# Two-layer hybrid decoder step: pooling and GLU columns as plain blocks, the gates as sevenfold products, and stores taken off the load queue

## The chip, the cores and the metric

The kernel runs on one core of a Trainium2 chip. The time is device microseconds of one execution of the whole program, read as the median of several runs; smaller is better. The engines are named as in the profile: PE is TensorE (matmul) and PEld its weight loads, DVE is VectorE, ACT is ScalarE, POOL is GpSimd, SP is SyncE, which here only issues DMAs. A name with a q (SPq, POOLq) is the engine's own DMA queue.

## The reference

One layer is applied to 1024 prompt tokens with 16 learned meta tokens ahead of them, and to 8 x 8 sample tokens, which carry their own states.

```python
h = rmsnorm(x)
a_val, a_gate, a_silu, p_in, p_silu, g_a, g_b = split(h @ w_in)     # seven groups of 1024 columns
u = a_val * sigmoid(a_gate)                                         # GLU
c = silu(layernorm(depthwise_conv(u, width=31) + conv_b)) * silu(a_silu)
br_a = c @ w_conv_out
pooled = trailing_mean(p_in, windows 2/4/8/16 by channel group) - p_in
q = (pooled @ w_pool_mix per group) * pool_scale * silu(p_silu)
br_b = q @ w_pool_out
y = rmsnorm(x + (sigmoid(g_a) * br_a + sigmoid(g_b) * br_b) @ w_out)
```

All is float32. The kernel also returns the last 30 GLU outputs and the last 15 pooling inputs as new states.

## The kernel before

**Layout.** Channels lie on the 128 partitions, tokens along the free axis. The 1104 tokens are cut into two halves of 552 (8 meta, 512 prompt, 32 sample). Each float32 operand of a matmul is split into a rounded high part and a low rest, and three matmuls (high-high, high-low, low-high) stand for one.

**Two ways to make a column group.** A column group is 128 output columns of `w_in`; there are 56. A *plain block* multiplies the group's 8 slices of 128 input channels with both token halves: 8 slices x 3 x 2 matmuls per half, 96 matmuls in all. A *sevenfold pair* makes two column groups at once with 7 products in place of 8 (the Strassen-Winograd scheme over 2 token halves x 2 halves of the channels x 2 column groups): each product is 4 slices x 3 x 2 = 24 matmuls, 168 for the pair instead of 192. It needs sums of weights (q3, q2, q1, q4) and sums of inputs (T1 to T4), and two combinations of results on DVE (`c4` and `c2`, lines 461 and 470). The product called `d` overwrites PSUM tile `v`, so it has to wait until DVE has read `v` for `c4`.

**The stages.** (1) Pooling columns p0 to p5 as plain blocks, while the RMS factor is worked out; their results go unscaled to DRAM (`d_raw`). (2) 25 sevenfold pairs: p3 (columns p6 and p7), g0 to g3 with v0 to v3 (GLU gates and values), and 16 pairs of gates q, b, a, s; `ORDER` gives the order. (3) `pmix`: the pooled channels times the group maps. (4) `ppo`: pool projection. LayerNorm statistics of the convolution are made beside it. (5) `pco`: conv projection and merge. (6) `pwo`: output projection and the final norm.

**What DVE does beside stage 2.** The pooling windows (`pool_window`) and the convolution (`conv_chunk`: for each of 8 channel chunks 31 taps over 1024 prompt tokens, and small sums for the sample tokens). These are kept in a list `todo`, and `fill` places as many of them between the products as a planned clock (3.0 us per product) leaves room for. The order on every engine is fixed when the program is written; each engine runs its own list in order and waits at semaphores.

**Weights of a product.** `prepare` loads a quarter of a pair's weights 8 products ahead on SP, adds a second quarter with an accumulating DMA from POOL 6 ahead (for q3 and q1), makes q2 and q4 on DVE 5 ahead, and splits 4 ahead with `split_dma`: two copies on ACT, then an accumulating DMA from POOL that subtracts the rounded part. All plain loads and all stores are issued by SP, in the order in which the program wrote them, a store as soon as its ACT instruction is written.

Of the kernel before, what the change touches and what calls it, by code (L numbers as in the profile page):

```python
# [65 lines left out]
def hybrid_trunk_kernel(  # L66
# [87 lines left out]

    def refine(r, a, t):
# [47 lines left out]
    d_raw = dram.tile([NX, P, 2, HT], F32, name="d_raw")  # L203
# [99 lines left out]
    d_rms = dram.tile([P, 2, HT], F32, name="d_rms")  # L303
    sp.dma_start(out=d_rms, in_=rms)
    keep_raw(0, 1, outs[0])

    t_ops = {}

    def t_split(name, k, src, how):
        t = slot(f"t{name}{k}", (2, HT), F32R)
        t_ops.setdefault(name, []).append(t)
        how(t[:, 0], t[:, 1], src)

    xa, xb = xs[:NQ], xs[NQ:]
    for k in range(NQ):
        dve.scalar_tensor_tensor(xa[k], xa[k], col(OFF_NG, k), rms, ALU.mult, ALU.mult)  # L320
        t_split("11", k, xa[k][:, 0], split)
        dve.scalar_tensor_tensor(xb[k], xb[k], col(OFF_NG, NQ + k), rms, ALU.mult, ALU.mult)
# [3 lines left out]
    for k in range(NQ):  # L326

        dve.tensor_tensor(xa[k][:, 0], xa[k][:, 0], xa[k][:, 1], ALU.subtract)
        dve.tensor_tensor(xa[k][:, 1], xb[k][:, 1], xa[k][:, 1], ALU.subtract)
        t_split("T3", k, xa[k][:, 1], split)  # L330
    plain1(3)
    plain1(4)
    plain1(5)
    keep_raw(2, 1, outs[2])

    def more_t(step):
        for k in range(NQ):
            if step == 0:
                t_split("21", k, xb[k][:, 0], split_dma)
            elif step == 1:  # L340
                dve.scalar_tensor_tensor(xa[k][:, 1], xa[k][:, 0], -1.0, xb[k][:, 1], ALU.mult, ALU.subtract)
                t_split("T2", k, xa[k][:, 1], split_dma)
            elif step == 2:
                t_split("T1", k, xa[k][:, 0], split)
            elif step == 3:
                t_split("22", k, xb[k][:, 1], split_dma)
            else:
                dve.scalar_tensor_tensor(xa[k][:, 1], xa[k][:, 1], -1.0, xb[k][:, 0], ALU.mult, ALU.subtract)
                t_split("T4", k, xa[k][:, 1], split)
# [3 lines left out]
    clock = {"pe": 0.0, "dve": 0.0}  # L353
# [16 lines left out]


    class Weights:
        def __init__(self, src, name):
            self.name = name
            (self.a_, self.b_), (self.c_, self.d_) = ((x[:, :NQ], x[:, NQ:]) for x in src)
            self.raw, self.op = {}, {}

        def load(self, what):
            src, key = {
                "a": (self.a_, "a"),  # L380
                "q3": (self.a_, "q3"),
                "q2": (self.c_, "q1"),
                "b": (self.b_, "b"),
                "d": (self.d_, "d"),
            }.get(what, (None, None))
            if key:
# [3 lines left out]
        def add(self, what):  # L390
            key, src = {"q3": ("q3", self.c_), "q2": ("q1", self.d_)}.get(what, (None, None))
            if key:
                pool.dma_start(out=self.raw[key], in_=src, accum_op=ALU.add)

        def sum(self, what):
            x, y = {"q2": ("q1", "a"), "q4": ("q2", "b")}.get(what, (None, None))
            if x:
                self.raw[what] = half_raw(f"{what}_{self.name}")
                dve.tensor_tensor(self.raw[what], self.raw[x], self.raw[y], ALU.add)
                spend(512)  # L400

        def split(self, what):
            o = op_tile(f"wo{what}_{self.name}", (2, NQ, P))
            split_dma(o[:, 0], o[:, 1], self.raw[what])
# [4 lines left out]
    def prepare(t):  # L409
        for lead, f in (  # L410
            (LEAD_LOAD, Weights.load),
            (LEAD_ADD, Weights.add),
# [7 lines left out]
    def product(out, w, t, units, first, last):  # L420
# [3 lines left out]
        clock["pe"] += T_PRODUCT  # L424
# [61 lines left out]


    def pool_window(j, e, es):
        sp.dma_start(out=o_pp[j], in_=e[:, TP - PB : TP])
        sp.dma_start(out=o_ps[j], in_=es[:, :, DS:])  # L490
        w = WINDOWS[j // 2]
        cur = [e, es]

        def step(d):
            lo = 2 * d - 1
            s, ss = cur
            cur[0] = slot(f"pw{j}_{d}", (TP,))
            cur[1] = st.tile([P, DB, PS], F32, tag="pws", name=f"pws{j}_{d}")
            dve.tensor_tensor(cur[0][:, lo:], s[:, lo:], s[:, lo - d : TP - d], ALU.add)
            dve.tensor_tensor(cur[1][:, :, lo:], ss[:, :, lo:], ss[:, :, lo - d : PS - d], ALU.add)  # L500

        work = []
        d = 1
        while d < w:
            work.append((t_op(TP) + t_op(DB * PS), lambda d=d: step(d)))
            d *= 2

        def last():
            s, ss = cur
            dve.scalar_tensor_tensor(e[:, META:], s[:, META:], 1.0 / w, e[:, META:], ALU.mult, ALU.subtract)  # L510
# [577 lines left out]
```

## Time and profile before

| what | value |
|---|---|
| median of 3 runs (lowest to highest) | 1257.62 us (1257.25 to 1264.47) |
| profiled execution: its own time, its span | 1264.1 us, 1262.3 us |
| PE, DVE, ACT, POOL busy | 1001.3, 719.7, 536.4, 278.4 us |
| mean granted TensorE clock | 0.888 |
| stage 1 | 0 to 81.9 us |
| stage 2 | 81.9 to 851 us |
| pmix, ppo, pco, pwo begin | 859, 905, 1040, 1158 us |

The page of the profile gives shares of the whole span, which mix the six stages. The table by stretch (busy time of every engine, granted clock, share of the 16 DMA engines' time) is the one to start from; then, for a stretch in which PE is not busy, the list of who waited for whom. A wait is put down to whatever came last, so a wait of PE for DVE has to be followed to what DVE waited for. In the 40 slices of the page PE is near full in the first two, at 1 to 7 tenths in the next eight, and at 5 to 9 from there on.

### The profile page before, as it was taken

What the parts mean: (1) busy time and instruction counts of PE and PEld (TensorE: products, weight loads), DVE (VectorE), ACT (ScalarE), POOL (GpSimd) and SP (SyncE); (2) the same over time, 40 slices, a digit from 0 to 9 for tenths busy, and PEclk for the clock granted to TensorE, in tenths of its full rate; (3) what the DMA queues carried; (4) which work ended last, traced back from release to release, by engine and by line L of the source; (5) the groups of instructions that cost most, each with busy time, mean ns of one, the idle gap of its engine ahead of it and who ended that gap; (6) DMA issues with size and microseconds to landing.
All of it is one profiled execution on the core that took longest, in us unless ns stands there. A gap on an engine that the chain in (4) does not pass through costs nothing. (4 is left out here: it accounts for less than half of the span.)

```text
span 1262.3 us, 18203 instructions
## 1 busy us (share of the span) xinstructions
PE 1001.3 (79%) x6960; PEld 967.7 (77%) x6960; DVE 719.7 (57%) x901; ACT 536.4 (42%) x928; POOL 278.4 (22%) x340
## 2 busy tenths in 40 slices
PE   9952516745898979898899879895897665999997
PEld 9952516634897979898889879895797665999885
DVE  6462335234796879676987689752624343446333
ACT  7535425333454555454545346441423543314111
POOL 0004233222333333333333333310011111100000
PEclk9986758767888989998999889897899787999999
DMA  7119889898989799979897989969962667855222
GB/s 259 63 62 191 197 152 181 197 173 168 235 213 206 126 231 220 217 133 214 198 234 113 216 180 230 212 165 352 354 168 81 175 166 192 244 144 185 86 81 100
DMA packets 146711, 230.66 MB, mean 183 GB/s; under 512 B 47936, under 2 KB 49344, under 8 KB 146624
## 3 DMA queue, kind: packets, MB, share of 16 engines
q1 hardware_dynamic: 104288, 149.98, 38.3%
q0 software_dynamic: 42336, 79.53, 36.7%
q8 instruction: 54, 0.88, 0.3%
q14 instruction: 33, 0.27, 0.1%
HBM read 116.77 MB, written 50.18 MB: 132 GB/s over the span
## 5 line engine op out<-in xcount | busy, mean ns | idle before, releaser
L606 DVE SCALAR_TENSOR_TENSOR c<-ce,pv,c 128x1024 f32<-128x1024 f32 x240 | 307.9, 1283 | 6.5
L146 PE MATMUL pco<-cx,w_co 128*128 128x272 f32 x768 | 101.7, 296 | 21.5 <-DMA w_co<-raw_co 10.8
L146 PEld LDWEIGHTS pco<-cx,w_co 128*128 128x128 f32 x768 | 100.5, 195 | 22.7 <-DMA w_co<-raw_co 11.3
L146 PE MATMUL ppo<-q,w_po 128*128 128x272 f32 x768 | 102.4, 297 | 5.5 <-DMA w_po<-raw_po 5.5
L146 PEld LDWEIGHTS ppo<-q,w_po 128*128 128x128 f32 x768 | 101.9, 197 | 6.0 <-DMA w_po<-raw_po 6.0
L961 PE MATMUL pwo<-wo,mx 128*128 128x512 f32 x336 | 79.2, 394 | 0.0
L961 PEld LDWEIGHTS pwo<-wo,mx 128*128 128x128 f32 x336 | 63.1, 188 | 14.7
L146 PE MATMUL pp<-xg,wh_p 128*128 128x276 f32 x384 | 65.9, 292 | 1.0 <-ACT rawp L242 0.6
L146 PEld LDWEIGHTS pp<-xg,wh_p 128*128 128x128 f32 x384 | 55.1, 189 | 2.5 <-DVE xg L195 0.9
L146 PE MATMUL pmix<-lp,m 128*128 128x272 f32 x192 | 33.3, 339 | 21.1 <-DMA lp<-d_pool 9.3
L146 PEld LDWEIGHTS pmix<-lp,m 128*128 128x128 f32 x192 | 31.0, 235 | 23.3 <-issue 16.2
L123 POOL DMA_DIRECT2D w_po<-raw_po x16 | 13.9, 867 | 140.1 <-ACT w_po L122 99.4
L550 DVE TENSOR_TENSOR pe<-lraw,lrms 128x512 f32<-128x512 f32 x12 | 8.3, 692 | 62.0 <-DMA lrms<-d_rms 62.0
L848 DVE TENSOR_TENSOR lb<-ppo,lb 128x544 f32<-128x544 f32 x16 | 11.5, 722 | 55.0 <-DMA lb<-d_sgb 41.7
L146 PE MATMUL pp<-xg,wl_p 128*128 128x276 f32 x192 | 40.0, 289 | 0.0
L146 PE MATMUL px_q<-tT,woq_q 128*128 128x272 f32 x192 | 28.3, 307 | 11.0 <-ACT c_q L437 10.7
L116 ACT CAST mx<-lga 128x544 fp32r<-128x544 f32 x16 | 10.3, 646 | 62.0 <-DVE lga L923 62.0
L943 ACT ACTIVATE sq<-xr 128x1024 f32<-128x1024 f32 (+1 forms) x9 | 8.7, 965 | 64.1 <-DVE xr L980 64.1
L146 PEld LDWEIGHTS px_q<-tT,woq_q 128*128 128x128 f32 x192 | 27.0, 206 | 11.4 <-ACT c_q L437 10.9
L146 PE MATMUL px_v<-tT,woq_v 128*128 128x276 f32 x192 | 28.1, 306 | 8.6 <-ACT c_v L437 8.6
L146 PEld LDWEIGHTS px_v<-tT,woq_v 128*128 128x128 f32 x192 | 27.2, 205 | 8.8 <-ACT c_v L437 8.8
L980 DVE TENSOR_TENSOR xr<-pwo,xr 128x1024 f32<-128x1024 f32 (+1 forms) x9 | 10.0, 1106 | 40.0 <-PE pwo L961 25.8
(414 smaller groups left out, 2417.5 us busy)
## 6 DMA issues: line engine op xcount, KB each, us to landing
d_pool<-poolop SPq DMA_DIRECT2D x16, 544.0 KB, 3.4
lp<-d_pool SPq DMA_DIRECT2D x16, 544.0 KB, 7.5
d_c<-c SPq DMA_DIRECT2D x8, 544.0 KB, 3.5
lg<-d_gate SPq DMA_DIRECT2D x16, 272.0 KB, 6.7
lb<-d_sgb SPq DMA_DIRECT2D x16, 272.0 KB, 6.4
lc<-d_c SPq DMA_DIRECT2D x8, 544.0 KB, 10.5
d_tb<-lb SPq DMA_DIRECT2D x16, 272.0 KB, 2.6
lsa<-d_sa SPq DMA_DIRECT2D x16, 272.0 KB, 6.9
```

Of the source, the lines that this page charges most:

```text
L116: act.copy(dst_h, src)
L123: pool.dma_start(out=dst_l, in_=src, accum_op=ALU.add)
L146: pe.matmul(out[:, u, : hi - lo], w(k, a), xs(k, b)[:, lo:hi], start=first and k == ks[0] and i == 0, stop=last and k == ks[-1] and i == 2 ...
L550: dve.tensor_tensor(o[1], r[1], f[1], ALU.mult)
L606: dve.scalar_tensor_tensor(c, s, wk[:, k : k + 1], c, ALU.mult, ALU.add)
L848: dve.tensor_tensor(of_half(lb[h]), ps, of_half(lb[h]), ALU.mult)
L943: act.activation(sq[:rows, c], xr[:, c], AF.Square, accum_out=a1 if ns[0] else a0)
L961: pe.matmul(ps[:, n - ns[0]], x(k), wo[k][n][w], start=(k == 0 and s == 0), stop=(k == NK - 1 and s == len(passes) - 1),)
L980: dve.tensor_tensor(v3(xr[:, c], 512), ps[:, : len(ns)], v3(xr[:, c], 512), ALU.add)
```

## The change

- Stage 2 becomes two phases. `BLOCKS`: p6, p7 and then g0, v0, ... g7, v7, 18 plain blocks. `ORDER`: the 16 pairs of gates stay sevenfold. The matmuls of stage 2 go from 25 x 168 = 4200 to 18 x 96 + 16 x 168 = 4416.
- Both token halves of the normalized input are split whole (`hx`, 16 tiles); T1 to T4 are made at the end of the blocks.
- A GLU result is not copied into the convolution's input by ACT and POOL: DVE multiplies, the result goes to DRAM (`d_e`, `d_es`), and `Conv.fetch` loads it back, at most two chunks at a time.
- The pooling work is planned in `todo` with everything it does; `d_rms` is gone, the RMS factor stays in SBUF; raw columns are loaded one chunk ahead (`pool_load`).
- All sums of weights are made on DVE (q3, q1, q2, q4) from four loaded quarters; the accumulating POOL loads are gone. q4 is split by ACT and DVE.
- Results of gates, `d_raw` and p columns are stored from ACT's queue. The other stores stay on SP, but `defer` writes them 1 to 3 steps later in the program.
- The first loads of pmix are written before the end of the last pair, and the stores of `d_tb` in ppo one half later.

Cut to its core:

```diff
-ORDER = "p3 g0 q0 q1 q2 g1 q3 b0 b1 g2 b2 b3 a0 g3 a1 a2 a3 s0 s1 s2 s3"
-LEAD_LOAD, LEAD_ADD, LEAD_SUM, LEAD_SPLIT = 8, 6, 5, 4
+BLOCKS = "p6 p7 " + " ".join(f"g{i} v{i}" for i in range(8))
+ORDER = "q0 q1 q2 q3 b0 b1 b2 b3 a0 a1 a2 a3 s0 s1 s2 s3"
+LEAD_LOAD, LEAD_SUM, LEAD_SPLIT = 8, 5, 4
+ON_DVE = ("q4",)
...
+    def defer(steps, run):
+        due.append((clock["step"] + steps, run))
+    def step(us):
+        clock["step"] += 1
+        clock["pe"] += us
+        for x in [x for x in due if x[0] <= clock["step"]]:
+            due.remove(x)
+            x[1]()
...
     def keep_raw(j, h, ps):
...
-        sp.dma_start(out=d_raw[j][:, h], in_=z)
+        act.dma_start(out=d_raw[j][:, h], in_=z)
...
+            self.src = {"a": ("a", a), "q3": ("c", c), "q2": ("d", d), "b": ("b", b)}
...
-        def add(self, what):
-            key, src = {"q3": ("q3", self.c_), "q2": ("q1", self.d_)}.get(what, (None, None))
-            if key:
-                pool.dma_start(out=self.raw[key], in_=src, accum_op=ALU.add)
         def sum(self, what):
-            x, y = {"q2": ("q1", "a"), "q4": ("q2", "b")}.get(what, (None, None))
+            sums = {"q3": (("q3", "a", "c"),), "q2": (("q1", "c", "d"), ("q2", "q1", "a")), "q4": (("q4", "q2", "b"),)}
+            for key, x, y in sums.get(what, ()):
+                self.raw[key] = half_raw(f"{key}_{self.name}")
+                dve.tensor_tensor(self.raw[key], self.raw[x], self.raw[y], ALU.add)
...
+            if what in ON_DVE:
+                split(o[:, 0], o[:, 1], self.raw[what])
+            else:
+                split_dma(o[:, 0], o[:, 1], self.raw[what])
...
             act.activation(o, z, func)
-            sp.dma_start(out=dst[2 * i + b][:, h], in_=flat(o))
+            act.dma_start(out=dst[2 * i + b][:, h], in_=flat(o))
...
+        else:                                   # a GLU value block
+            z = sg.pop(h)
+            dve.tensor_tensor(v3(z, HT // 2), ps, v3(z, HT // 2), ALU.mult)
+            def out():
+                sp.dma_start(out=d_e[i][:, META + h * HP : META + (h + 1) * HP], in_=p)
+                sp.dma_start(out=d_e[i][:, h * HM : (h + 1) * HM], in_=m)
+                sp.dma_start(out=d_es[i][:, h * DB // 2 : (h + 1) * DB // 2], in_=s)
+            defer(1, out)
...
+        def fetch(self):
+            sp.dma_start(out=e[:, CB:], in_=d_e[i])
+            sp.dma_start(out=es[:, :, :CB], in_=sconv[i])
+            sp.dma_start(out=es[:, :, CB:], in_=d_es[i])
+            defer(3, lambda: sp.dma_start(out=o_cp[i], in_=e[:, TP : TP + CB]))
...
+    for n, (kind, i) in enumerate(blocks):
+        if n + 2 < len(blocks):
+            ops[n + 2].load()
+        if n + 1 < len(blocks):
+            ops[n + 1].split()
+        if left in (3, 2):
+            make_t(3 - left, split_dma)
...
+            gemm(ps, ops[n], lambda k, s: hx[h][k][:, s], UNITS1, every, True, True)
+            put_block(kind, i, h, ps[:, :, : HT // 2])
+            step(2 * T_PRODUCT)
...
+            if left > 1:
+                fill(clock["pe"])
...
+            load_mix(0)                         # during the last pair
+            load_gate(0)
+            load_pooled(0)
+            load_pooled(1)
...
-            sp.dma_start(out=d_tb[d][:, h], in_=lb[h])
+            defer(1, lambda d=d, h=h, z=lb[h]: sp.dma_start(out=d_tb[d][:, h], in_=z))
```

**SP in the middle of stage 2.** First the queue of SP before, around the gates b0 and b1 (`b_b`, `a_b`, `q_b`, `d_b` are quarters of their weights, `d_gate` and `d_sgb` stores of gate results, `d_c` of a convolution chunk).

```order
L388 DMA b_b_3445<-in_w_in 128x512
L586 DMA d_gate<-zq_3512 128x544
L388 DMA a_b_3523<-in_w_in 128x512
L623 DMA d_c<-c_2868 128x1088
L388 DMA d_b_3598<-in_w_in 128x512
L586 DMA d_gate<-zq_3628 128x544
L388 DMA q_b_3635<-in_w_in 128x512
L586 DMA d_gate<-c_q_3555 128x544
L388 DMA q_b_3668<-in_w_in 128x512
L586 DMA d_gate<-c_q_3476 128x544
L388 DMA b_b_3706<-in_w_in 128x512
L586 DMA d_sgb<-zb_3771 128x544
```

In the change the same place of SP's queue reads:

```order
L399 DMA b_b_4495<-in_w_in 128x512
L399 DMA a_b_4562<-in_w_in 128x512
L399 DMA c_b_4679<-in_w_in 128x512
L399 DMA d_b_4712<-in_w_in 128x512
L605 DMA ce_4747<-d_e 128x1040
L606 DMA ces_4748<-in_sconv 128x8x30
L607 DMA ces_4748<-d_es 128x8x8
L399 DMA b_b_4758<-in_w_in 128x512
L644 DMA d_c<-c_4001 128x1088
L399 DMA a_b_4827<-in_w_in 128x512
```

The gates' stores, which stood between any two loads, are gone from SP; what is left between the loads comes once per convolution chunk.

**DVE over one pair of gates in the change**, from one `c4` combination to the next (`c` is the convolution, `q..` the sums of weights, `woq4` the low part of q4):

```order
L470 SCALAR_TENSOR_TENSOR c4_b0_4863<-pv_b0_4711,c4_b0_4863 128x544
L621 SCALAR_TENSOR_TENSOR c4_4753<-ce4_3995,pv_74,c4_4753 128x2x512 x3
L405 TENSOR_TENSOR q4_b1_4969<-q2_b1_4831,b_b1_4758 128x512
L479 SCALAR_TENSOR_TENSOR c2_b0_4787<-pv_b0_4711,c2_b0_4787 128x544
L621 SCALAR_TENSOR_TENSOR c4_4753<-ce4_3995,pv_74,c4_4753 128x2x512 x3
L120 TENSOR_TENSOR woq4_b1_5007<-q4_b1_4969,woq4_b1_5007 128x512
L621 SCALAR_TENSOR_TENSOR c4_4753<-ce4_3995,pv_74,c4_4753 128x2x512 x2
L405 TENSOR_TENSOR q3_b2_5038<-a_b2_4827,c_b2_4934 128x512
L621 SCALAR_TENSOR_TENSOR c4_4753<-ce4_3995,pv_74,c4_4753 128x2x512 x2
L405 TENSOR_TENSOR q1_b2_5075<-c_b2_4934,d_b2_4967 128x512
L405 TENSOR_TENSOR q2_b2_5077<-q1_b2_5075,a_b2_4827 128x512
L621 SCALAR_TENSOR_TENSOR c4_4753<-ce4_3995,pv_74,c4_4753 128x2x512 x2
```

Two of the four sums and the low part of q4 are new on DVE here; twelve taps of the convolution fill the rest of the pair.

## Rows read from the trace of the kernel before

**Rows 1.** The page: DMA queues (packets, MB, share), and one issue's time to landing.

```profile
q1 hardware_dynamic: 104288, 149.98, 38.3%
q0 software_dynamic: 42336, 79.53, 36.7%
woq_g<-q_g POOLq DMA_DIRECT2D x16, 256.0 KB, 4.9
```

**Rows 2.** Busy time by stretch of the span, all engines; the first line names the columns.

```profile
core 0: us, PE busy (x) PEld busy (x) DVE busy (x) ACT busy (x) POOL busy (x), PEclk, DMA share, GB/s
81.90:306.00 224.10, 101.43 (x628) 98.58 (x628) 78.42 (x137) 95.92 (x181) 65.81 (x85) 0.70 0.86 176
...
452.50:851.00 398.50, 360.64 (x2688) 357.20 (x2688) 308.56 (x332) 194.46 (x336) 132.09 (x156) 0.94 0.90 197
851.00:905.30 54.30, 33.19 (x194) 31.05 (x193) 21.24 (x30) 13.44 (x22) 1.73 (x2) 0.78 0.94 335
905.30:1035.00 129.70, 106.30 (x786) 104.69 (x784) 53.30 (x58) 52.07 (x69) 15.65 (x18) 0.89 0.59 170
```

**Rows 3.** PE in order of time: start, us, instruction; stage 1, then gates s.

```profile
50.48 0.68 PE L146 MATMUL pp<-xg,wh_p 128*128 128x276 f32 x4
...
74.07 0.68 PE L146 MATMUL pp<-xg,wh_p 128*128 128x276 f32 x4
...
782.25 3.18 PE L146 MATMUL pv_s<-tT,woq_s 128*128 128x272 f32 x24
...
797.32 3.16 PE L146 MATMUL px_s<-t,woq_s 128*128 128x272 f32 x24
```

**Rows 4.** Waits of PE, 81.9 to 306: us in total, times, longest.

```profile
PE pv_p L146 <- DVE c_p L461: 32.8, 1, 32.8
PE px_v L146 <- ACT c_v L437: 26.9, 2, 18.3
...
PE px_p L146 <- ACT woa_p L121: 12.3, 1, 12.3
```

**Rows 5.** Waits of DVE, 81.9 to 306.

```profile
DVE pe L550 <- DMA lrms<-d_rms: 62.0, 10, 12.7
```

**Rows 6.** Waits, 306 to 851: DVE (first and last of five groups), and PE's longest.

```profile
DVE q_a L399 <- DMA q_a<-in_w_in: 24.8, 3, 10.6
...
DVE q_s L399 <- DMA q_s<-in_w_in: 6.7, 2, 5.2
...
PE pv_q L146 <- DVE c_q L461: 13.2, 3, 6.2
```

**Rows 7.** Groups of instructions by form: busy us, mean ns, idle before.

```profile
L606 DVE SCALAR_TENSOR_TENSOR c<-ce,pv,c 128x1024 f32<-128x1024 f32 x240 | 307.9, 1283 | 6.5
L614 DVE TENSOR_TENSOR tap<-ces,pv 128x248 f32<-128x248 f32 x64 | 23.5, 409 | 0.0
L617 DVE TENSOR_REDUCE c<-tap 128x16 f32<-128x496 f32 x32 | 21.4, 670 | 1.1
...
L499 DVE TENSOR_TENSOR pw<-pe 128x1039 f32<-128x1039 f32 x8 | 9.9, 1235 | 1.9 <-POOL pe L551 1.9
...
L399 DVE TENSOR_TENSOR q_a<-q_a,a_a 128x512 f32<-128x512 f32 x4 | 2.8, 691 | 24.8 <-DMA q_a<-in_w_in 24.8
```

**Rows 8.** SP's queue in order of time: start, us, issue; gates, then ppo.

```profile
458.88 0.33 SPq L586 DMA_DIRECT2D d_gate<-c_q  x1
459.30 0.98 SPq L388 DMA_DIRECT2D b_b<-in_w_in  x1
...
964.81 11.97 SPq L849 DMA_DIRECT2D d_tb<-lb  x2
```

**Rows 9.** Waits, 851 to 1041: PE's longest two, and one of DVE.

```profile
PE pt_v L170 <- ACT sumh_v L116: 13.0, 1, 13.0
PE pmix L146 <- DMA lp<-d_pool: 9.3, 2, 8.0
...
DVE lb L848 <- DMA lb<-d_sgb: 34.1, 4, 9.5
```

More of the change, by code (lines that the diff above doesn't have):

```diff
@@ L302, in hybrid_trunk_kernel, with split_x @@
     rms = inv_root(xtot, HT, RMS_EPS, "x")
-    d_rms = dram.tile([P, 2, HT], F32, name="d_rms")
-    sp.dma_start(out=d_rms, in_=rms)
     keep_raw(0, 1, outs[0])
[L311 to L322, printed above, removed]
+    hx = [[], []]
+    def split_x(h, ks, how):
+        for k in ks:
+            t = slot(f"hx{h}{k}", (2, HT), F32R)
+            how(t[:, 0], t[:, 1], xs[k][:, h])
+            hx[h].append(t)
+    for k in range(NK):
+        dve.scalar_tensor_tensor(xs[k], xs[k], col(OFF_NG, k), rms, ALU.mult, ALU.mult)
+        split_x(0, (k,), split)
     plain1(1)
@@ L325, in hybrid_trunk_kernel @@
     keep_raw(1, 1, outs[1])
[L326 to L330, printed above, removed]
+    split_x(1, (0, 1), split)
     plain1(3)
+    keep_raw(2, 1, outs[2])
+    split_x(1, (2, 3), split)
     plain1(4)
+    keep_raw(3, 1, outs[3])
+    split_x(1, (4, 5), split)
     plain1(5)
[L334 to L349, printed above, removed]
+    keep_raw(4, 1, outs[4])
+    split_x(1, (6, 7), split)
     todo = deque()
-    clock = {"pe": 0.0, "dve": 0.0}
     def spend(n, count=1):
@@ L368, in fill, with __init__, load, split @@
             run()
+    class Block:
+        def __init__(self, src, name):
+            self.name, self.src = name, src
+        def load(self):
+            self.raw = [half_raw(f"raw{b}_{self.name}") for b in range(2)]
+            for b in range(2):
+                sp.dma_start(out=self.raw[b], in_=self.src[:, b * NQ : (b + 1) * NQ])
+        def split(self, how=split_dma):
+            self.op = []
+            for b in range(2):
+                o = op_tile(f"w{b}_{self.name}", (2, NQ, P))
+                how(o[:, 0], o[:, 1], self.raw[b])
+                self.op.append(o)
+        def __call__(self, k, s):
+            return self.op[k // NQ][:, s, k % NQ]
     class Weights:
@@ new lines, in hybrid_trunk_kernel, with __init__, more, taps @@
+    d_es = dram.tile([NK, P, DB, DS], F32, name="d_es")
+    class Conv:
+        fetched = []
+        def __init__(self, i):
+            self.i = i
+            work = [(t_op(SEQ) if k else 0.75, lambda k=k: self.taps(k)) for k in range(CW)]
+            work += [(1.5, lambda b=b: self.sample(b)) for b in range(0, DB, 2)]
+            push(work + [(0.0, self.store)])
+            chunks.append(self)
+            Conv.more()
+        @staticmethod
+        def more():
+            for x in chunks:
+                if len(Conv.fetched) < 2 and not hasattr(x, "e"):
+                    Conv.fetched.append(x)
+                    x.fetch()
+        def fetch(self):
+            i = self.i
+            e = self.e = slot(f"ce{i}", (CB + TP,))
+            es = self.es = st.tile([P, DB, ES], F32, tag="ces", name=f"ces{i}", bufs=2)
+            pool.memset(e[:, :CB], 0.0)
+            sp.dma_start(out=e[:, CB:], in_=d_e[i])
+            sp.dma_start(out=es[:, :, :CB], in_=sconv[i])
+            sp.dma_start(out=es[:, :, CB:], in_=d_es[i])
+            defer(3, lambda: sp.dma_start(out=o_cp[i], in_=e[:, TP : TP + CB]))
+            defer(3, lambda: sp.dma_start(out=o_cs[i], in_=es[:, :, DS:]))
+        def taps(self, k):
+            i = self.i
+            wk = col(OFF_CW, i * CW + k)
+            s = v3(self.e[:, META + k : TP + k], HP)
@@ L683, in hybrid_trunk_kernel @@
     pairs = []
-    for step in ORDER.split():
-        for r1, r2, name, units, put in steps[step[0]](int(step[1])):
+    for name in ORDER.split():
+        for r1, r2, name, units, put in steps[name[0]](int(name[1])):
             w = Weights((r1, r2), name)
```

343 lines of the change are left out of this document (151 added, 192 removed).

## The prediction

> **What bounds the kernel now.** I read the busy times by stretch first, then the waits in the stretches where PE is not busy, then the order in time of the queue that the waits point to.
>
> The table by stretch [rows 2] splits stage 2 in two. From 81.9 to 306 PE is busy 101.4 of 224.1 us at a granted clock of 0.70, so most matmuls there also run at the lower of the two levels, 1.2 GHz. From 452.5 to 851 it is busy 360.6 of 398.5 us at 0.94. At the full clock a product of 24 matmuls takes (797.32 - 782.25) / 5 = 3.01 us, and 31 groups of 6 matmuls with 276 columns take 74.07 - 50.48 = 23.59 us, 0.127 us each [rows 3]. Stage 2 holds 175 products, 527 us, and takes 769: 242 us are lost, the largest sum anywhere in the kernel. What I want to know is which of these 242 us the change can reach.
>
> In the early stretch PE waits for DVE and ACT once for 32.8 and twice for 26.9 us [rows 4]. They are not slow: DVE is busy 78 of 224 us. DVE itself waits 62.0 us in ten pieces for the RMS factor that is read back from DRAM for every pooling chunk [rows 5], a load that stands on SP behind everything else. Since DVE runs its list in order, a combination that PE needs is stuck behind a pooling chunk that needs a load.
>
> In the late stretch the waits of DVE for the sums of weights (q_a to q_s, five groups, 24.8 the longest and 6.7 the shortest [rows 6]) stand first. Such a sum reads what an accumulating POOL load has written. PE's longest waits there are the `d` products, which wait for `c4` on DVE (13.2 us in the gates q alone [rows 6]). The queue of SP shows the other half: a load of weights is issued at 459.30, directly after a store that went out at 458.88 [rows 8] and that had to wait for its ACT instruction.
>
> **The change part by part.**
>
> *Matmuls.* 18 plain blocks of 96 matmuls at 0.127 us are 219 us, 16 pairs of 7 products at 3.01 us are 337 us. Stage 2 needs 556 us of full-clock PE time after, 527 before: **+29 us**, all of it on the path wherever PE is the limit.
>
> *The beginning.* PE idles 12.3 us after 81.9 for the first split weights [rows 4]. The first block needs its own weights and inputs that DVE and ACT scale and split one after the other, twice as many as before. I keep 12.3; bounds 5 (one accumulating DMA's landing, 4.9 [rows 1]) and 25 (twice as many splits).
>
> *DVE.* After the pooling its list holds 240 taps at 1.283 (308 us), 64 small products at 0.409 with 32 reductions at 0.670 (48), and at 0.69 each [rows 7] 64 sums of weights (44), 16 low parts of q4 (11), 32 combinations (22), 16 GLU products (11) and 24 steps for T (17): 461 us. Pooling needs 28 wide steps at 1.235 and 16 scalings at 0.69, with some 40 small steps at 0.3 (an estimate from the 0.409 above) 57 us. Together 518 us against 556 of PE: DVE is nearly full, and the plan fills every pair of gates with it. That decides how much slack is left.
>
> *Pooling without the read-back of the RMS factor.* One chunk took 224 / 8 = 28 us before, since each needs four loads in turn. After, two remain, issued one chunk ahead. DVE's own part is 57 / 8 = 7 us a chunk. I take 11 us, 88 for all, since splitting, landing and storing of one chunk overlap only the next; bounds 7 and 28. Pooling then ends at 94 + 88 = 182, and DVE is through with the rest at 182 + 461 = 643 plus its own waits. PE alone would be at 94 + 556 = 650.
>
> *Waits that stay.* Before, pairs of gates lost (398.5 - 16 x 21.1) / 16 = 3.8 us each [rows 2, 3]. The sums no longer wait for POOL's accumulating loads, and the loads no longer wait behind the gates' stores. New per pair on DVE are two sums and a low part, 2.1 us. I leave 1.6 us a pair for late combinations, 25 us, bounds 0 and 4.5 a pair (72). For the blocks I leave 20 us: weights of the block after next are split on ACT behind the pooling's splits, so a late pooling chunk holds up PE; bounds 0 and 60. Stage 2 then ends at 94 + 556 + 45 = 695, against 851: **-156 us**, already with the +29.
>
> *GLU through DRAM.* Each chunk writes and rereads half a megabyte. Its price lies on SP: a store waits for DVE's product, and the load of weights for the block after next stands behind it. With two blocks (24 us) of lead against a landing and a split of about 10, I cost it at nothing as long as DVE is less than some 12 us late.
>
> *pmix.* PE waits 9.3 us for pooled channels [rows 9], and the DMA engines are 0.94 busy at 335 GB/s [rows 2], while 192 matmuls need 24 us of 54. The stage is bound by what it loads. Two of eight chunks and one gate are now loaded before the last pair ends: about 4 MB of 18 (335 GB/s times 54.3 us). I take **-13**, bounds 4 and 20.
>
> *ppo and the start of pco.* DVE waits 34.1 us for `lb` [rows 9], because the loads stand behind `d_tb` stores that hold SP for 11.97 us at a time [rows 8]. With the stores one half later these loads go out in time, the squares are ready sooner and PE's 13.0 us at the variance [rows 9] go. What is late next is the eight chunks after the root, which pco needs at once: I give half of it back. **-11**, bounds 3 and 22.
>
> **Sum.** 1264.1 us is the profiled execution's own time, 1.8 over its span. 1264.1 - 156 - 13 - 11 = 1084. That execution is 6.5 us (0.5%) above the median of 1257.62 that the change is compared with, so I forecast **1080 us**.
>
> **The rivals.**
>
> *The sixteen DMA engines become the bound (17%).* They are 0.90 busy from 452.5 to 851 [rows 2], 22.4 us a pair against PE's 21.1. From the page, accumulating DMAs cost 36.7% of 1262 us for 79.5 MB, 5.8 us per MB, plain ones 38.3% for 150 MB, 3.2 [rows 1]. A pair of gates loses three accumulating quarters (4.6 us) and one load (0.8) and comes to 18 us, which fits. But a pooling chunk moves two loads, two accumulating pieces and two stores, 9 us, and the block beside it 4.7 us of every 12.2: at full engines 9 / (1 - 0.39) = 15 us a chunk, 120 for all. Then DVE ends 32 us later, of which the slack takes some: about 1105. The Trainium skill (DMA: Bandwidth & Descriptors, "Issuing engines are not separate DMA queues") says that transfers started by ScalarE, SyncE or GpSimd run on the same 16 engines, and that a second issuer saves only the time to issue. By that rule the stores on ACT's queue save 64 x 0.33 = 21 us of SP's issuing [rows 8] and no transfer time. The trace of before has no store on ACT's queue; against the rule as the whole account stands that the store's cost there is SP's waiting, not its issuing.
>
> *DVE or ACT is the limit in the gates (13%).* DVE's 21 us of planned work per pair leaves nothing, and ACT now also waits until each store's source is written. If 3 us more are lost per pair, as much as before the change, the time is 1080 + 48 = 1128.
>
> *The reordering doesn't free the pooling (4%).* If a chunk keeps the 28 us of before, stage 2 gets 8 x 17 = 136 us longer: 1216.
>
> *Slower than before (3%).* In the blocks SP holds three things that wait for DVE (GLU stores, pooling stores, reloads of the convolution) ahead of loads that PE and DVE need, so lateness could feed itself. DVE has about 200 us of work in the 220 us of blocks. Before, from 81.9 to 306, it was busy 35% of the time; were it so here, the blocks would take 570 us and the kernel 1430. The change becomes slower where DVE is busy for less than about half of the block phase (400 us). Against it speaks that each of these stores is written 6 to 18 us later than its source, which none was before.
>
> **How the numbers follow.** My forecast has 63%, its own range is 1050 to 1110. With the bounds of the terms and the first two rivals the range is **1040 to 1140**; the rest is outside on both sides. What a measurement can tell from no change is about 1%, 13 us. Every case but the last is faster by more than that: faster 0.95, same 0.02, slower 0.03.
>
> **What would show it.** After, the block phase should begin near 95 and take 230 to 245 us with the granted clock above 0.9; a pooling chunk should take about 11 us; DVE's waits for sums of weights should be gone, and DVE over 85% busy from the first tap to the end of the gates; pmix should take about 41 us, and the wait at the variance should be gone while one appears at the start of pco. The forecast fails if PE waits in the blocks for split weights again and again, or if a pair of gates takes 24 us or more.

## The result and the profile after

The changed kernel takes **1114.92 us** (median of 4 runs, 1111.57 to 1117.58) against 1257.43 before: ratio 0.886, 95% interval 0.881 to 0.890. It is faster by 142 us. Forecast were 1080 us, 177 less; the time lies inside the range and 35 us above the forecast, just outside the likeliest case's own 1050 to 1110.

The profiled execution took 1117.6 us (span 1115.8). The table by stretch of the changed kernel answers to [rows 2]; the columns are the stretch, its length, busy time of each engine with the number of instructions, the granted clock, the DMA share and GB/s. The blocks run up to 363, the gates to 713, the mixing product to 762, the product with `w_po` to 894.

```profile
81.90:121.00 39.10, 34.10 (x240) 33.66 (x241) 15.40 (x32) 21.20 (x39) 7.09 (x8) 0.91 0.78 164
121.00:260.00 139.00, 105.13 (x740) 103.56 (x739) 82.63 (x131) 43.80 (x84) 28.39 (x35) 0.89 1.03 206
260.00:363.00 103.00, 101.99 (x801) 101.77 (x801) 96.11 (x105) 33.06 (x56) 20.12 (x24) 1.00 0.71 163
363.00:713.00 350.00, 342.03 (x2686) 340.50 (x2685) 315.54 (x366) 195.22 (x325) 88.54 (x104) 0.99 0.85 201
713.00:762.00 49.00, 31.90 (x197) 29.90 (x195) 20.52 (x29) 12.56 (x21) 1.72 (x2) 0.79 0.98 352
762.00:894.00 132.00, 103.91 (x785) 102.20 (x786) 55.34 (x61) 56.10 (x75) 16.84 (x20) 0.92 0.58 166
...
94.00:220.50 126.50, 96.50 (x682) 95.16 (x683) 53.08 (x116) 43.35 (x86) 25.64 (x31) 0.90 1.04 199
220.50:713.40 492.90, 478.58 (x3732) 476.61 (x3732) 447.72 (x501) 239.55 (x399) 116.64 (x138) 0.98 0.83 193
```

Read it by the third column, PE's busy time. The gates keep PE busy for 342 of 350 us. From 121 to 260 it is busy for only 105 of 139, and there the DMA engines are full (1.03) while they move 206 GB/s. The last two rows cut stage 2 at VectorE's last pooling instruction: pooling takes 126.5 us, 15.8 a chunk, and everything behind it 492.9.

The order of time, set against the sum that was predicted (both on the profiled executions, 1084 forecast and 1117.6 measured):

| Term | Forecast | Measured | Error, us |
|---|---|---|---|
| Blocks, from 94 | 239 | 268.9 | +30 |
| Gates | 362 | 350.5 | -11.5 |
| Mixing product, against 54.3 | -13 | -5.7 | +7 |
| Product with `w_po` up to PE's start on the last product (134.3 before, 131.8 after) | -11 | -2.5 | +8.5 |
| All behind | 0 | -0.7 | -1 |

The sum of the errors is 33. The waits that replaced those of [rows 4, 5] stand in the list of waits of the changed kernel between 121 and 363 (PE) and 121 and 260 (the others): engine, line, what was waited for, us in total, times, longest.

```profile
PE pv L149 <- DMA w_v<-raw_v: 20.7, 5, 7.9
PE pg L149 <- DMA w_g<-raw_g: 14.2, 3, 7.8
...
DVE pws L537 <- DMA pes<-in_spool: 32.6, 6, 11.7
...
POOL ce L604 <- DMA poolop<-pw: 9.5, 1, 9.5
POOL ce L604 <- DMA out<-pe: 7.3, 1, 7.3
...
ACT poolop L124 <- DMA out<-pe: 10.3, 1, 10.3
```

PE waits for weights of blocks. VectorE waits for the state of the pooling, and GpSimd and ScalarE each stand once or twice for about as long as PE at an instruction ahead of work on those weights (their longer waits in total, for VectorE and for each other inside the pooling, are left out here). That looks like a fault of order on three lists. The experiments show that it is only partly one.

### The profile page after: what moved, and what is told of

Same layout as the page of the kernel before. It is cut to its first block, busy times and chain, and to the rows that moved or that the text cites. A ratio compares the mean times of both kernels' runs of the same rounds, so it can differ in the third digit from the quotient of the medians.

```text
span 1115.8 us, 18229 instructions
## 1 busy us (share of the span) xinstructions
PE 990.3 (89%) x7176; PEld 962.1 (86%) x7176; DVE 731.9 (66%) x945; ACT 469.1 (42%) x791; POOL 174.4 (16%) x211
## 5 line engine op out<-in xcount | busy, mean ns | idle before, releaser
L149 PE MATMUL pv<-hx,w_v 128*128 128x276 f32 x768 | 105.1, 299 | 20.7 <-DMA w_v<-raw_v 20.7
L149 PEld LDWEIGHTS pv<-hx,w_v 128*128 128x128 f32 x768 | 103.2, 197 | 21.8 <-DMA w_v<-raw_v 21.8
L149 PE MATMUL pco<-cx,w_co 128*128 128x272 f32 x768 | 101.6, 295 | 22.4 <-DMA w_co<-raw_co 11.4
L149 PE MATMUL pg<-hx,w_g 128*128 128x276 f32 x768 | 104.5, 298 | 14.2 <-DMA w_g<-raw_g 14.2
L149 PEld LDWEIGHTS pg<-hx,w_g 128*128 128x128 f32 x768 | 103.0, 197 | 14.9 <-DMA w_g<-raw_g 14.9
L149 PE MATMUL ppo<-q,w_po 128*128 128x272 f32 x768 | 100.0, 293 | 6.4 <-DMA w_po<-raw_po 6.0
L149 PEld LDWEIGHTS ppo<-q,w_po 128*128 128x128 f32 x768 | 99.2, 192 | 7.2 <-DMA w_po<-raw_po 6.4
L993 PEld LDWEIGHTS pwo<-wo,mx 128*128 128x128 f32 x336 | 63.1, 188 | 14.8
L878 DVE TENSOR_TENSOR lb<-ppo,lb 128x544 f32<-128x544 f32 x16 | 11.5, 722 | 52.0 <-DMA lb<-d_sgb 40.2
L663 ACT ACTIVATE zg<-pg 128x552 f32<-128x552 f32 x16 | 9.9, 628 | 68.8 <-PE pg L149 63.3
L124 ACT CAST poolop<-pw 128x512 fp32r<-128x512 f32 x16 | 9.9, 618 | 60.8 <-DVE pw L542 33.1
```

What stands on the lines that cost most here:

```text
L124: act.copy(dst_h, src)
L149: pe.matmul(out[:, u, : hi - lo], w(k, a), xs(k, b)[:, lo:hi], start=first and k == ks[0] and i == 0, stop=last and k == ks[-1] and i == 2 ...
L663: act.activation(v3(sg[h], HT // 2), ps, AF.Sigmoid)
L878: dve.tensor_tensor(of_half(lb[h]), ps, of_half(lb[h]), ALU.mult)
L993: pe.matmul(ps[:, n - ns[0]], x(k), wo[k][n][w], start=(k == 0 and s == 0), stop=(k == NK - 1 and s == len(passes) - 1),)
```

## Experiments

All are made from the changed kernel. Their ratios are to the kernel before; 0.001 is 1.25 us.

**Which part won the gates?** Two parts of the change were undone, one at a time. First the gates' stores went back among the loads.

```diff
-            act.dma_start(out=dst[2 * i + b][:, h], in_=flat(o))
+            sp.dma_start(out=dst[2 * i + b][:, h], in_=flat(o))
```

> One part of the change undone: the stores of the gates are issued on SyncE's queue again, among the loads of weights, and no longer on ScalarE's. Theory 'waiting': a store holds SyncE until the activation before it is done, the loads behind it come late, and this was the larger part of what the gates gained (from 3.8 us lost per pair to 0.8): the 16 pairs take 25 to 50 us longer, 1140 to 1165 us. Rival 'sums': the gain of the gates came from the sums of weights that no longer wait for accumulating loads; loads are issued eight products (24 us) ahead, which covers a store's wait, so nothing changes by more than 5 us: 1112 to 1120.

Measured: 1111.49 us, ratio 0.886 (0.882 to 0.890), the same. The gates took 349.7 us, as this row from its table by stretch shows:

```profile
361.50:711.20 349.70, 342.13 (x2690) 340.50 (x2689) 316.42 (x367) 189.93 (x326) 87.95 (x104) 0.99 0.84 200
```

Then two sums of weights per pair went back to accumulating loads.

```diff
+        def add(self, what):
+            if what in self.acc:
+                key, src = self.acc[what]
+                pool.dma_start(out=self.raw[key], in_=src, accum_op=ALU.add)
...
-            sums = {"q3": (("q3", "a", "c"),), "q2": (("q1", "c", "d"), ("q2", "q1", "a")), "q4": (("q4", "q2", "b"),)}
+            sums = {"q2": (("q2", "q1", "a"),), "q4": (("q4", "q2", "b"),)}
```

> One part of the change undone: two of the sums of weights of each pair are made by accumulating loads on GpSimd's queue again (a third load of a quarter and two accumulating ones per pair), two sums per pair leave VectorE (1.4 us). Theory 'sums': VectorE waits again for these landings and holds up combinations behind it; PE loses 2 to 3 us per pair more, 30 to 50 us: 1145 to 1165 us. Rival 'waiting': the loads of these sums were late only because SyncE stood at the gates' stores; with the stores on ScalarE's queue the accumulating loads come in time, and the kernel takes 1110 to 1122 us.

Measured: 1154.0 us, ratio 0.919 (0.914 to 0.923), about 40 us slower. The row by stretch and the waits of VectorE in the gates:

```profile
361.60:753.90 392.30, 353.06 (x2690) 348.40 (x2690) 302.30 (x341) 197.05 (x327) 114.55 (x135) 0.97 0.93 217
```

```profile
DVE q_q L411 <- DMA q_q<-in_w_in: 16.7, 3, 7.8
DVE q_a L411 <- DMA q_a<-in_w_in: 16.0, 3, 10.4
```

The gates grow from 350.5 to 392.3 us, the waits of [rows 6] are back, and the DMA share rises from 0.85 to 0.93. In this run SyncE does not stand at the stores, and the loss is back; in the run before it stands there, and nothing is lost. So the sums on VectorE won the gates, and the rival "waiting" is out for this kernel. Whether the stores would matter together with the old sums was not run, and the 40 us are not divided between the landings that VectorE waits for and the fuller DMA engines.

**The product with `w_po`.** The list of SyncE is the same in both kernels. Of the order of the instructions, before and after, around the second chunk's loads:

```
before                        after
d_tb<-lb  (half 0)            d_tb<-lb  (half 0)
d_tb<-lb  (half 1)            d_tb<-lb  (half 1)
raw_po<-in_w_po  x2           raw_po<-in_w_po  x2
lb<-d_sgb  x2                 lb<-d_sgb  x2
```

A store that is put off by one step runs at the end of the step that is just being closed, right where it stood. The order in time of SyncE's queue (start, us, line, transfer, count) shows it still held for 11.97 us, as in [rows 8], and the waits between 762 and 900 are those of [rows 9]:

```profile
820.65 11.97 SPq L879 DMA_DIRECT2D d_tb<-lb  x2
832.72 0.93 SPq L374 DMA_DIRECT2D raw_po<-in_w_po  x2
833.71 1.62 SPq L727 DMA_DIRECT2D lb<-d_sgb  x2
```

```profile
DVE lb L878 <- DMA lb<-d_sgb: 40.2, 5, 9.1
...
PE pt_v L187 <- ACT sumh_v L119: 13.2, 1, 13.2
```

```diff
-            defer(1, lambda d=d, h=h, z=lb[h]: sp.dma_start(out=d_tb[d][:, h], in_=z))
+            defer(2, lambda d=d, h=h, z=lb[h]: sp.dma_start(out=d_tb[d][:, h], in_=z))
```

> In the product with w_po the stores of d_tb are put off by two half steps instead of one. In the changed kernel one step is no delay: the list of SyncE has the two stores of a chunk ahead of the loads of the next one exactly as before the change. Theory: with a true delay the loads of the gate of the next chunk go out one product (about 6 us) sooner, VectorE's waits for them (40.2 us in five pieces between 762 and 900) fall to under 15, PE's wait at the variance (13.2 us) goes, and part of it comes back at the start of the last product, where the eight chunks after the root are needed: 5 to 11 us less, about 1107. Rival: the squares and the root are paced by ScalarE and VectorE themselves, and the wait at the variance stays: 0 to 2 us, about 1114.

Measured: 1081.1 us, ratio 0.8635 (0.861 to 0.866), 28 us less than the change, far more than expected. SyncE's queue, the stretches (the product with `w_po`, then the last product) and the waits of this kernel:

```profile
804.23 0.95 SPq L879 DMA_DIRECT2D d_tb<-lb  x2
805.28 2.30 SPq L374 DMA_DIRECT2D raw_po<-in_w_po  x2
807.63 1.76 SPq L727 DMA_DIRECT2D lb<-d_sgb  x2
```

```profile
756.60:866.20 109.60, 101.49 (x784) 100.33 (x784) 56.93 (x63) 55.75 (x74) 16.63 (x20) 0.98 0.77 225
866.20:976.20 110.00, 102.25 (x769) 101.82 (x770) 51.49 (x73) 37.93 (x61) 11.17 (x13) 0.92 0.67 182
```

```profile
DVE lb L878 <- PE ppo L149: 23.6, 5, 8.8
...
PE pt_v L187 <- DVE suml_v L120: 1.9, 1, 1.9
```

At the same place in the list a pair of stores now takes 0.95 us of the queue and not 11.97 (the seven pairs of the stage together 30.9 and not 65.0), VectorE waits for PE's product instead of the load, and PE waits 1.9 us at the variance instead of 13.2. The stage goes from 131.8 to 109.6 us and the last product from 117.4 to 110.0. The mechanism was the expected one; the size was not, because `raw_po`, `raw_co` and the loads of the last branch stand behind the same stores: PE's idle time in the stage falls from 28 to 8 us and its clock rises from 0.92 to 0.98.

**The mixing product.** The changed kernel shows one transfer behind others in the order in time of SyncE, VectorE and PE (the number in brackets is the idle time before the row, with what ended it). PE waits for VectorE's gating product `lg`, which stands in VectorE's list behind the split of the weights (`mraw`) that SyncE issued after pooled chunks and gates:

```profile
722.78 0.38 SPq L749 DMA_DIRECT2D mraw<-in_w_mix  x1
...
729.73 0.69 DVE L120 TENSOR_TENSOR m<-mraw,m 128x512 fp32r<-128x512 f32 x1 [15.39 <-ACT m L119]
...
731.22 9.03 PE L149 MATMUL pmix<-lp,m 128*128 128x272 f32 x48 [9.49 <-DVE lg L840]
```

```diff
...
+            load_mraw(0)
+            load_mraw(1)
             load_mix(0)
...
+        if j in (0, 2):
+            load_mraw(j // 2 + 2)
```

> The weights of each quarter of w_mix are loaded one quarter earlier (256 KB each; the second already in the last pair of gates); the splits stay where they were. Theory 'order of the loads': in the changed kernel PE waits 9.5 us in the mixing product because the second quarter's weights are issued at 722.8 us behind four pooled chunks and two gates and land at 729; issued sooner, this wait goes and the stage from 713 to 762 shrinks by 6 to 9 us: about 1107 us. Theory 'DMA engines full': the engines are busy 0.98 of this stage at 352 GB/s, so what is loaded sooner makes the pooled chunks later by as much: 0 to 2 us, about 1114.

Measured: 1107.52 us, ratio 0.883 (0.8795 to 0.886); the stage took 45.6 us instead of 48.6. The row by stretch and the waits of PE:

```profile
705.50:751.10 45.60, 29.72 (x194) 28.41 (x193) 20.54 (x29) 12.45 (x21) 1.72 (x2) 0.81 1.02 378
```

```profile
PE pmix L149 <- DMA lp<-d_pool: 8.9, 4, 3.9
PE pmix L149 <- DVE lg L848: 6.8, 1, 6.8
...
ACT w_po L124 <- DMA raw_po<-in_w_po: 9.6, 1, 9.6
```

The wait goes and comes back in two parts: 8.9 us for pooled channels, with the DMA engines full at 378 GB/s, and 6.8 us behind VectorE. By the waits the second part is again one of order: VectorE waits for ScalarE, which stands 9.6 us at weights of the next product (last row). Moving the loads was worth 3 us; how the rest divides between full engines and order is not told apart. The total differs by more than the stage, but its interval overlaps that of the change.

**The blocks.** Three ways to get weights to PE sooner: loads and splits one block ahead, low parts on VectorE, clearing by a DMA on SyncE.

```diff
+    ops[2].load()
+    ops[1].split()
...
-            ops[n + 2].load()
+            ops[n + 3].load()
...
-            ops[n + 1].split()
+            ops[n + 2].split()
```

> The weights of a block are loaded three blocks ahead instead of two and split two ahead instead of one; nothing else moves. Theory 'order of the lists': in the changed kernel a block's weights stand in an in-order list behind an instruction that waits for something else (on ScalarE behind pooling outputs, on GpSimd behind the clearing of a convolution tile, on SyncE behind a reload of the GLU), and one block of lead (12 us) more covers each of these waits (4 to 8 us). PE's five gaps in the blocks (32.8 us) and the lower clock after them (about 12 us) go, the block phase from about 94 to 363 shrinks by 30 to 40 us, and the kernel takes about 1080 us. Theory 'DMA engines full': from 121 to 260 us the sixteen engines are busy for the whole time, so weights that come sooner make pooling later by as much; the phases up to the end of the gates give back at most 10 us and the kernel takes 1105 us or more.

```diff
-            ops[n + 1].split()
+            ops[n + 1].split(split if n < 12 else split_dma)
```

> The weights of the first twelve blocks after the first are split with the low part on VectorE, so 24 accumulating DMAs of 256 KB go and VectorE gets 24 subtractions of 0.69 us (17 us, of about 60 that it is idle there). Theory 'DMA engines full': 24 x 128 packets x 178 ns / 16 engines = 34 us of engine time less, the DMA share between 121 and 260 us falls to 0.85 or lower, the landings get shorter, a pooling chunk takes 12 us instead of 15.7, the block phase shrinks by 20 to 30 us: about 1090 us. Theory 'order of the lists': GpSimd's list is out of the way of the weights (two gaps of PE, 7.9 and 4.1 us), those behind ScalarE and SyncE stay and VectorE's own waits (for pooling's state and for GLU reloads) now hold weights up too: 1105 to 1120 us.

```diff
...
-            pool.memset(e[:, :CB], 0.0)
+            sp.dma_start(out=e[:, :CB], in_=zeros)
```

> The 30 columns ahead of a convolution chunk are cleared by a small DMA on SyncE's queue from a tile of zeros, ahead of the reload that waits for the same tile, and no longer by a memset on GpSimd, where the accumulating DMAs for the weights' low parts stand behind it. Theory 'order of the lists': GpSimd no longer waits 7.3 and 9.5 us there, PE's gaps before two of the value blocks (7.9 and 4.1 us) and the lower clock after them (about 2.4 us each) go, 12 to 17 us: about 1100 us. Theory 'DMA engines full': the low parts land no sooner, since the transfers ahead of them take the engines: 0 to 4 us, about 1113.

Measured: 1106.76 (ratio 0.8835, 0.880 to 0.887), 1110.70 (0.886, 0.884 to 0.889) and 1111.20 us (0.888, 0.884 to 0.891). None differs clearly from the change. Neither theory stands as it was written: the order of the lists alone gave less than 10 us, and so did the DMA time that the second edit takes away. In the run with more lead the waits of PE between 121 and 363 were these:

```profile
PE pv L149 <- DVE zg L666: 14.8, 3, 6.7
PE px_q L149 <- DMA woa_q<-a_q: 7.3, 1, 7.3
PE pv L149 <- DMA w_v<-raw_v: 2.6, 1, 2.6
```

The weights come in time, and PE waits for VectorE's GLU products, which free the buffers that it writes to, and at the first gate. The blocks end at 345.4 there and not at 362.9, but the pooling only 1.9 us and the gates 8.8 us sooner. So the state of the pooling, VectorE's longest wait, came next.

```diff
+            lpes[j] = st.tile([P, DB, PS], F32, tag="pes", name=f"pes{j}", bufs=4)
+            sp.dma_start(out=lpes[j][:, :, :PB], in_=spool[j])
...
-            sp.dma_start(out=es[:, :, :PB], in_=spool[j])
```

> The state of a pooling chunk (60 KB in pieces of 60 bytes) is loaded one chunk ahead, with the chunk's raw block, into one of four buffers instead of two; nothing else moves. Three loads of weights, low parts and a memset moved out of the way, one at a time, have left the block phase within 7 us of its 269, and PE's gaps came back at another engine's door, so a common cause is looked for. Theory 'pooling is a chain': VectorE waits 32.6 us in six pieces between 121 and 260 for that state, everything behind it on VectorE (GLU products that free PE's banks, pooling outputs that ScalarE waits for ahead of weights) is late for that reason; without the wait a chunk takes 11 to 12 us instead of 15.7, PE's gaps shrink by half or more, and the phase by 15 to 30 us: 1085 to 1100 us. Theory 'DMA engines full' (share 1.0 to 1.1 between 121 and 250): the wait moves to the next landing, 0 to 7 us: 1108 to 1115 us.

(Of the three runs before, the one with more lead had shortened the blocks by 17.5 us, not 7: its first gate began at 345.4 and then waited 7.3 us.) Measured: 1106.09 us, ratio 0.883 (0.879 to 0.887), by the ratios 3.5 us less than the change, as the second theory says. The wait is gone, and VectorE's longest between 94 and 220 is another:

```profile
DVE poolop L120 <- ACT poolop L119: 45.1, 16, 12.3
DVE pw L537 <- DMA out<-pe: 8.2, 1, 8.2
```

> Both edits together: the state of a pooling chunk one chunk ahead, and the weights of the blocks one block sooner. Theory 'pooling is a chain': with the weights out of the way too, PE has no gap left that another list makes, the block phase takes 235 to 245 us instead of 269: 1080 to 1090 us. Theory 'DMA engines full': the sum of what each edit gave alone, 0 to 10 us: 1105 to 1115 us.

Measured: 1096.56 us, ratio 0.875 (0.872 to 0.879), between the two theories.

> As the run with the two edits, and the low parts of the first blocks' weights on VectorE as well (22 accumulating DMAs of 256 KB less, about 31 us of engine time by 178 ns a packet). Theory 'DMA engines full': neither edit alone helped since the freed time was in the wrong resource each time; with the engines relieved and the chain shortened at once the block phase takes 230 to 240 us: 1075 to 1088 us, and 20 us or more less than the run without this third edit. Theory 'pooling is a chain': no more than 5 us less than the run without the third edit.

Measured: 1091.05 us, ratio 0.871 (0.868 to 0.874), some 5 us below the run without the third edit, nearer to the chain's forecast and outside both. The blocks took 237.5 us there, from 94 to 331.5. By the ratios the three edits together took 18 us off the change (0.886 to 0.871), where each alone gave 0 to 4.

> All edits that gave something alone or together: pooling state and weights of the blocks sooner, low parts of the first blocks' weights on VectorE, weights of the mixing product sooner, and the stores in the product with w_po put off by a true half step. Theory: the gains lie in different stages and add: 1091 us of the run with the three edits on the blocks, less the 28 to 34 us that the stores' delay gave and the 3 to 7 of the mixing weights: about 1056 us (1050 to 1062). Rival: the earlier stages end sooner and the same loads meet fuller DMA engines, so a third of it is lost: 1066 us or more.

Measured: 1059.03 us, ratio 0.850 (0.844 to 0.856), as the sum says. This version beats both kernels; by the ratios it is 4% faster than the change. The last run took VectorE's waits for ScalarE at the pooled outputs, 24.9 us in the run before, out of the pooling:

```diff
+    def split_own(dst_h, dst_l, src):
+        dve.tensor_copy(dst_h, src)
+        dve.tensor_tensor(dst_l, src, dst_h.bitcast(F32), ALU.subtract)
...
-            split(v3(o[:, 0, HP:], DS), v3(o[:, 1, HP:], DS), ss[:, b, PB:])
+            split_own(v3(o[:, 0, HP:], DS), v3(o[:, 1, HP:], DS), ss[:, b, PB:])
```

> As the run with all edits, and the sample part of a pooled chunk (128x32) is rounded and split by VectorE alone, so that its list no longer waits there for ScalarE, which works through casts of weights ahead of it. In all versions so far the gates end 484 to 494 us after VectorE's last pooling instruction, whatever was moved in the blocks. Theory 'VectorE is behind from the pooling on': VectorE's 28 us of waits for ScalarE in the pooling (run with three edits) go, the pooling ends 10 to 20 us sooner and the gates with it: 1038 to 1050 us. Theory 'DMA engines full': pooling goes on at 13 us a chunk, the wait moves to a landing: 0 to 4 us less than the run with all edits.

Measured: 1057.69 us, ratio 0.850 (0.842 to 0.857), the same as without it. Its last pooling instruction started at 200.0; the rows are cut at VectorE's first tap, 200.9, and below them stands VectorE's longest wait before it:

```profile
94.00:200.90 106.90, 104.28 (x797) 104.28 (x798) 66.88 (x155) 34.03 (x58) 14.14 (x18) 0.97 0.99 206
200.90:687.50 486.60, 463.79 (x3618) 461.98 (x3617) 451.69 (x508) 233.73 (x388) 108.80 (x129) 0.98 0.80 190
...
DVE w_v L120 <- ACT w_v L119: 10.5, 2, 7.9
```

ScalarE is busy for a third of the pooling and VectorE for 63%, while the DMA share is 0.99. The pooling is 2 us shorter; VectorE's waits for landings grew from 13.5 to 27.1 us, as the rival said, and those for ScalarE's casts of weights from 7.0 to 14.9.

One number links these runs. The start of VectorE's last pooling instruction, the end of the gates, and the difference, us:

| Version | Pooling ends | Gates end | Between | PE busy between |
|---|---|---|---|---|
| the change | 220.5 | 713.4 | 492.9 | 478.6 |
| more lead | 218.6 | 704.6 | 486.0 | 469.8 |
| zeros by DMA | 215.3 | 707.1 | 491.8 | 475.4 |
| low parts on VectorE | 211.2 | 705.6 | 494.4 | 475.5 |
| state ahead | 211.1 | 702.9 | 491.8 | 477.7 |
| state ahead, more lead | 210.2 | 693.9 | 483.7 | 468.5 |
| all three block edits | 201.2 | 688.7 | 487.5 | 463.4 |
| all edits | 202.2 | 688.6 | 486.4 | 463.4 |
| all edits, own split | 200.0 | 687.5 | 487.5 | 464.7 |

The gates end 484 to 494 us after the pooling whatever else is moved. PE's own work fills 95 to 97% of that time in every version, so the constant alone does not show that the pooling sets the end. In the change PE has that much left because it was starved before. Where PE was fed in time its idle time came back at the first gate. In the last version VectorE's list there reads (taps, then the subtractions that make the operands T), and on GpSimd's the first gate's weights stand behind these operands:

```profile
325.21 9.21 DVE L626 SCALAR_TENSOR_TENSOR c<-ce,pv,c 128x1024 f32<-128x1024 f32 x7
...
336.90 0.73 DVE L700 TENSOR_TENSOR ts<-x,x 128x552 f32<-128x552 f32 x1
```

```profile
333.88 0.87 POOL L130 DMA_DIRECT2D tT<-ts  x1 [3.22 <-issue]
335.97 0.86 POOL L130 DMA_DIRECT2D woa_q<-a_q  x1 [1.22 <-DVE q_q L409]
```

```profile
PE px_q L153 <- DMA woa_q<-a_q: 7.7, 1, 7.7
```

VectorE was busy for 87.85 of the 90 us from 250 to 340 there. So it carries the lateness of the pooling on, and PE, when nothing else holds it, runs into it. This is read from the lists and the waits; no run ended the pooling clearly sooner with PE fed all the time.

## Why the prediction was right and where it was wrong

**Sign and size.** Right: 142 us of the 177 forecast came, most of it in stage 2 (-137.6 of the forecast -156). Of the 137.6, 48.0 lie in the gates (398.5 us before, 350.5 after), and a run shows what won them. The other 89.6 lie ahead of the gates (370.6 us from 81.9 to 452.5 before, 281.0 after, from 81.9 to 362.9). There the waits for the RMS factor, 62.0 us before, are gone, but no run undid the plain blocks, the RMS factor's place or the way of the GLU, so how these 89.6 us divide among them is argued and not shown.

**Matmuls, beginning.** The matmuls were priced rightly; the granted clock was 0.89 from 121 to 260 and 1.00 from there to the end of the blocks. The beginning is right by luck. The blocks were under way at 95.5, but the idle time of 12.3 us that led there is another one than was forecast (PE's waits, 40 to 97):

```profile
PE pp L149 <- ACT rawp L259: 7.7, 1, 7.7
PE pp L149 <- DMA w_p<-raw_p: 3.9, 1, 3.9
```

The 7.7 us lie ahead of the last half of the pooling columns, which began at 82.3: ScalarE's copy out of a bank that PE needed stood behind its casts of the inputs. For the first block's weights PE waited 4.6 us (the 3.9 and 0.7 for ScalarE).

**Gates.** Right in mechanism, and better than forecast: (350.5 - 337) / 16 = 0.8 us lost per pair, where 1.6 were kept. The sums did it, as the run with the old sums shows. The part of the argument that gave SyncE's waiting at the stores a price was wrong for these sums: moved back, the stores cost nothing. The Trainium skill (DMA: Bandwidth & Descriptors, "Issuing engines are not separate DMA queues") states that transfers started by different engines share the same DMA engines, so that a second issuer saves issuing time alone. The traces agree: the gates took 349.7 us with the stores on SyncE's queue and 350.5 without, so not even the 21 us of issuing were on the path.

**Pooling.** This is the step that failed. "I take 11 us" a chunk; it took 15.8, and pooling ended at 220.5 and not 182. VectorE's own part was well sized (53.1 us measured, with some GLU products among it, 57 forecast; 447.7 behind it, 461 forecast). What was missed was the rival's arithmetic: it gave 15 us a chunk at full DMA engines, and the share was 1.04. Its price, 1105 us for the whole, lies nearest to the measured time. (In its sum for a pair of gates, 22.4 - 4.6 - 0.8 is 17.0 and not 18; 0.85 of 350 us is 18.6 a pair.) Full engines are not the whole cause. The poolings of three runs: low parts on VectorE, state ahead with more lead, and all three block edits:

```profile
94.00:211.20 117.20, 97.61 (x701) 96.72 (x702) 63.95 (x137) 35.46 (x74) 14.17 (x18) 0.90 0.90 191
94.00:210.20 116.20, 102.74 (x768) 101.88 (x768) 52.90 (x118) 45.74 (x90) 27.15 (x33) 0.93 1.07 219
94.00:201.20 107.20, 103.81 (x803) 103.59 (x804) 64.20 (x137) 36.85 (x76) 15.07 (x19) 0.98 0.99 205
```

Length times share is the engines' time: about 131 us in the change, 105, 124 and 106 here. In the first run the engines were no longer full and the pooling still took 117 us, so a chain of waits held it; in the second they were full; both edits together took 19 us off it, where each had taken 9 or 10. So far as these rows go, each of the two causes holds the pooling when the other is relieved; the first edit also took work off GpSimd's list, and that part isn't separated. The cause of the last 107 us stays open: the engines are full again, but no run took out transfers of the pooling itself, and none moved ScalarE's copies of the first blocks' results, which in the last version waited 14.8 us for PE, ahead of casts for the pooling.

**Waits in the blocks.** The mechanism was named (weights held up behind the pooling's splits), the size was not: 268.9 us against 239, so 50 us were lost and not 20. It is not just the pooling's error seen on PE: with all three block edits the blocks took the forecast time, 237.5 us, while the pooling still took 107 and not 88. PE then waited 14.3 us in the first gate, and the gates took 357.2.

**pmix.** Wrong by 7 us: 48.6 us, not 41. A quarter's weights were left behind the pooled chunks (3 us by the run that moved them); the rest is divided between transfers at full engines and ScalarE's order, in shares that no run shows.

**ppo and the start of pco.** The step itself was wrong: "with the stores one half later" was read off the number in the code and not off the order of the list, which hadn't changed. The -2.5 us came without it. The mechanism was right, and undersized: the true delay gives 28 us.

**What would show it.** The waits for the sums were gone (0.2 us left) and VectorE was 91% busy from the first tap to the end of the gates, as said. The block phase and the chunk missed, and PE's wait at the variance stayed at 13.2 us; of the two signs of failure one came (PE waiting again and again in the blocks), the other, 24 us per pair, did not.

## What to carry to other kernels

Where a change claims to move an instruction, find it in the order of its queue before pricing the move. Where several engines wait in turn for about the same time, moving one of them out of the way moves the gap. Here each of three edits on the blocks gave 0 to 4 us and all together 18, so run them together before dropping them. An interval that stays the same through all versions is a lead, but first see how much of it is the work of the engine that sets the pace. Price a stage against the DMA engines' busy share, since here they were full at little more than half of the bandwidth that they reached elsewhere.

## What the runs showed of the hardware

The sixteen DMA engines were as busy from 94 to 220 (1.04, 199 GB/s) as in the mixing product (0.98, 352 GB/s). By queue in the first of these stretches (packets, MB, share of 16 engines), with two kinds of transfer (count, KB each, us from issue to landing):

```profile
q1 hardware_dynamic: 26712, 15.93, 60.4%
q0 software_dynamic: 4227, 7.71, 36.4%
...
d_pool<-poolop SPq DMA_DIRECT2D x12, 544.0 KB, 7.7
```

Per MB that is 126.5 x 0.604 / 15.93 = 4.8 us on the plain queue and 6.0 on the accumulating one; 22,192 of all 31,668 packets were under 512 bytes, but by the packets' own times in the trace these took only 20 of the engines' 131 us; the larger plain packets took 65 us for 16.1 MB, 4.1 us per MB, where in the mixing product they took 2.7. From 94 to 260, a state of 60 KB in pieces of 60 bytes took 10.4 us to land as a store, longer than the 544 KB of a pooled chunk at 7.9.
